# Weights, h and g in SBUF: tiles that begin at one place within 512 bytes, or at several

## The chip, the cores and the metric

The kernel runs on one core of one Trainium2 chip. The metric is the device time of one execution in microseconds, the median of several runs. A profiled execution is one run that the hardware profiler recorded; it has its own time.

## The reference: what is computed

One decoder layer on a sequence of 512 tokens with 1024 channels, in float32:

```
h = modulate(rmsnorm(x, g_ffn1), sh1, sc1)
x = x + 0.5 * gt1 * (silu(h @ w1_gate) * (h @ w1_up)) @ w1_down        # 1024 -> 2816 -> 1024
h = modulate(rmsnorm(x, g_mix), sh2, sc2)
x = x + gt2 * mixer(h)            # one input projection, convolution and sparse attention, one output projection
h = modulate(rmsnorm(x, g_ffn2), sh3, sc3)
x = x + 0.5 * gt3 * (silu(h @ w2_gate) * (h @ w2_up)) @ w2_down
out = rmsnorm(x, g_final)
```

The nine vectors sh, sc and gt come from `silu(c) @ w_ada`, 37.7 MB of weights for one vector c. Almost all the arithmetic is in the two feed-forward parts.

## The kernel before, in words

Activations stand transposed: channels on the 128 partitions, the 512 tokens along the row. Every float32 product is made from float32r parts. A weight block w is split into `whi` (rounded) and `wlo` (the rest), an activation into `hhi` and `hlo`, or `ghi` and `glo` behind the gate. `mm3` (L280) then issues three matmuls for each half of the tokens: hi by hi, low activation by hi weight, hi activation by low weight. Each one has 128 columns of weights to load and 256 columns of activations to stream, and each has its own weight load.

Weights come in units of 1024 columns, 4096 bytes a partition. A unit lands in one of four `raw` tiles, ScalarE rounds it into `whi` (L372), VectorE or GpSimd subtracts to make `wlo` (L361). There are four pairs `whi0..3`, `wlo0..3` (L333), taken in turn. Two further pairs, `whik` and `wlok` (L591), are allocated in the pool of a feed-forward part behind g and hold its last two units. In the mixer the last two units are held in `PT` tiles instead. h is eight pairs of 512 columns, 2048 bytes a partition (L513); g is eleven such pairs (L587).

`project` goes through the eight channels' blocks d of h with one unit of weights: six matmuls for d = 0, six for d = 1, and so on. `part` does the same over the eleven blocks of g, with a unit change every eight. The same weight tile therefore stands against each h tile in turn.

Tiles are laid into a partition's row one after the other in the order in which they are declared. All of these have sizes that are multiples of 512 bytes, so all weights begin at one place within 512 bytes, all h tiles at one place, and all g tiles at one place. Between the weights and h, `cact`, `mod`, `am` and `gb` (L416 to L419) take 112 float32, 448 bytes. Within 512 bytes, h then begins 64 bytes before the place of the weights. As the program is laid out: weights at byte 448, h, g, `whik` and `wlok` at 384, the first four `PT` at 256 and a fifth at 160.

The order of the instructions on each engine is settled when the program is built, by a planner (`Plan`, with costs such as `c_mm3`) that knows nothing of addresses. In the first feed-forward part the 56 tiles of `w_ada` are loaded as well (`araw`), and VectorE adds them up (L871).

Of the kernel before, what the change touches and what calls it, by code (L numbers as in the profile page):

```python
# [10 lines left out]
F32 = mybir.dt.float32  # L11
F32R = mybir.dt.float32r
# [7 lines left out]
P = 128  # L20
T = 512
D = 1024
DK = D // P
F = 2816
FK = F // P
FH = FK // 2
# [7 lines left out]
UNIT = 1024  # L34
# [26 lines left out]
N_RAW, N_W, N_SCR = 4, 4, 6  # L61
# [74 lines left out]
class Plan:  # L136
# [12 lines left out]
    def go(self, rank, task):  # L149
        self.n += 1  # L150
        self.step([rank, self.n, task, [self.at], None], None)
# [8 lines left out]
    def give(self, slots, i, at=None):  # L160
        slots.idle.append((*(at or self.at), i))
        able = [w for w in slots.waiters if w[4] < len(slots.idle)]
        if able:
            w = min(able, key=lambda w: w[:2])
            slots.waiters.remove(w)
            self.step(w, self.take(slots, w))
# [52 lines left out]
def c_act(n):  # L219
    return ACT, 0.1 + 0.84e-3 * n  # L220


def c_tt(n):
    return DVE, 0.07 + 1.04e-3 * n


def c_stt(n):
    return DVE, 0.13 + 1.04e-3 * n
# [14 lines left out]
def c_mm3(n):  # L243
    return PE, 3 * max(n / 2370, 0.105)
# [11 lines left out]
def tile_hymba_layer(ctx: ExitStack, tc: tile.TileContext, xT, pos, cols_d, con_d, wa0, wa1, f1a, f1b, f1d,  # L256
# [3 lines left out]
    const = ctx.enter_context(tc.tile_pool(name="const", bufs=1))  # L260
# [12 lines left out]
    small_of = [const.tile([P, 3, NB, 2], F32, name=f"v{i}") for i in range(8)]  # L273
    small = Slots(range(8))


    def mm(o, lhsT, rhs, start, stop):
        nc.tensor.matmul(o, lhsT, rhs, start=start, stop=stop)  # L278

    def mm3(o, w, x_, start, stop):  # L280

        n = o.shape[-1]
        wide = n == T and x_[0].shape[-1] == T
        halves = HALVES if wide else (slice(0, n),)
        for ts in halves:
            x0, x1 = (x_[0][:, ts], x_[1][:, ts]) if wide else x_
            o_ = o[:, ts] if wide else o
            mm(o_, w[0], x0, start and ts is halves[0], False)
            mm(o_, w[0], x1, False, False)
            mm(o_, w[1], x0, False, stop and ts is halves[-1])  # L290
# [39 lines left out]
    units += ffn_units(f2a, f2b, f2d)  # L330

    raw_of = [const.tile([P, UNIT], F32, name=f"raw{i}") for i in range(N_RAW)]
    whi_of = [const.tile([P, UNIT], F32R, name=f"whi{i}") for i in range(N_W)]  # L333
    wlo_of = [const.tile([P, UNIT], F32R, name=f"wlo{i}") for i in range(N_W)]
    raws, ws = Slots(range(N_RAW)), Slots(range(N_W))
    loaded, made = [Event() for _ in units], [Event() for _ in units]
    raw_at, w_at = {}, {}
# [40 lines left out]
    def take_unit():  # L378
        used[0] += 1
        return used[0] - 1  # L380

    def cols(u, j, n=P):
        i = w_at[u]
        return whi_of[i][:, j * n:(j + 1) * n], wlo_of[i][:, j * n:(j + 1) * n]

    def free_unit(u):
        give(slots_of.get(u, ws), w_at[u])
# [122 lines left out]
            if self.uses[i] == DK and self.copied is None:  # L510
                give(banks, self.bank[i])

    hhi = [const.tile([P, T], F32R, name=f"hhi{d}") for d in range(DK)]  # L513
    hlo = [const.tile([P, T], F32R, name=f"hlo{d}") for d in range(DK)]

    def h_of(d, ts=FULL):
        return hhi[d][:, ts], hlo[d][:, ts]
# [17 lines left out]
    def residual(d, b, gate, ts, norm):  # L535
        n = ts.stop - ts.start
        yield c_stt(n)
        nc.vector.scalar_tensor_tensor(x[d][:, ts], bank_of[b][:, ts], gate, x[d][:, ts], op0=OP.mult, op1=OP.add)  # L538
        give(banks, b)
        yield from norm.add(d, ts)  # L540

    def project(b):

        u = take_unit()
        yield made[u]
        for d in range(DK):
            yield c_mm3(T)
            mm3(bank_of[b], cols(u, d), h_of(d), d == 0, d == DK - 1)
        free_unit(u)
# [34 lines left out]


    def ffn(s, gp, accs, norm, end):
        ghi = [gp.tile([P, T], F32R, name=f"ghi{k}") for k in range(FH)]  # L587
        glo = [gp.tile([P, T], F32R, name=f"glo{k}") for k in range(FH)]
        sg_of = [gp.tile([P, T], F32, name=f"sg{k}") for k in range(2)]
        for k in range(KEEP[s]):  # L590
            whi_of.append(gp.tile([P, UNIT], F32R, name=f"whik{k}"))  # L591
            wlo_of.append(gp.tile([P, UNIT], F32R, name=f"wlok{k}"))
            give(kept[s], len(whi_of) - 1)
        sgs, gs = Slots(range(2)), [Slots([k]) for k in range(FH)]
        g_in = [Event() for _ in range(FK)]
        gate = [mod[:, 3 * s + 2, d:d + 1] for d in range(DK)]
        at = {}

        def glu(f, bg, bu):
            k = yield sgs  # L600
            yield c_act(T)
            nc.scalar.activation(sg_of[k], bank_of[bg], AF.Silu)
            give(banks, bg)
            q = yield scr
            yield c_tt(T)
            nc.vector.tensor_mul(scr_of[q], sg_of[k], bank_of[bu])  # L606
            give(banks, bu)
            give(sgs, k)
            j = yield gs[f % FH]
            yield c_act(T)  # L610
            nc.scalar.activation(ghi[j], scr_of[q], AF.Copy)  # L611
            yield c_tt(T)
            nc.vector.tensor_sub(glo[j], scr_of[q], ghi[j].bitcast(F32))  # L613
            give(scr, q)
            done(g_in[f])

        def part(half, d, b, ts, keep=False):
            for k in range(FH):
                n = d * FH + k
                if (half, n // 8) not in at:  # L620
                    at[half, n // 8] = take_unit()
                u = at[half, n // 8]
                yield made[u]
                yield g_in[half * FH + k]
                yield c_mm3(ts.stop - ts.start)
                mm3(bank_of[b][:, ts], cols(u, n % 8), (ghi[k][:, ts], glo[k][:, ts]), k == 0, k == FH - 1)
                if n % 8 == 7 and not keep:
                    free_unit(u)
                if half == 0 and d == DK - 1:
                    give(gs[k], k)  # L630

        def first_half(d, b):
            yield c_stt(T)
            nc.vector.scalar_tensor_tensor(x[d], bank_of[b], gate[d], x[d], op0=OP.mult, op1=OP.add)
            give(banks, b)

        def main():
            for f in range(GRP):
                go(R_GLU, glu(f, accs[2 * f], accs[2 * f + 1]))
            for f in range(GRP, FK):  # L640
                if f == FH:
                    for d in range(DK):
                        b = yield banks
                        yield from part(0, d, b, FULL)
                        if d == 0:
                            yield mod_in[3 * s + 2]
                        go(R_X, first_half(d, b))
                bg = yield banks
                yield from project(bg)
                bu = yield banks  # L650
                yield from project(bu)
                go(R_GLU, glu(f, bg, bu))
            for d in range(DK - 2):
                b = yield banks
                yield from part(1, d, b, FULL)
                go(R_X, residual(d, b, gate[d], FULL, norm))
            for ts in HALVES:
                for d in (DK - 2, DK - 1):
                    b = yield banks
                    yield from part(1, d, b, ts, True)  # L660
                    go(R_X, residual(d, b, gate[d], ts, norm))
            for n in range(8, FH):
                free_unit(at[1, n])
            done(end)

        go(R_MAIN, main())
# [289 lines left out]
    with tc.tile_pool(name="g0", bufs=1) as gp:  # L956
        go(R_ADA, ada_loads())
        go(R_ADA, ada_sums())
        go(R_TAB, rope_tables())
        parts = start_builds(1, norm)  # L960
        ffn(0, gp, accs, norm, end)
        plan.run(end)
        plan.run(mod_in[8])
        plan.run(tables_in)
# [3 lines left out]
    with ExitStack() as mixer:  # L968
# [634 lines left out]
        n = 0  # L1603
# [105 lines left out]
    with tc.tile_pool(name="g2", bufs=1) as gp:  # L1709
# [54 lines left out]

        squared = norm.squared
        ffn(2, gp, accs, norm, end)
        for d in range(DK):
            go(R_Y, final(d))
# [130 lines left out]
```

## Time and profile before

| | |
|---|---|
| three runs | 1066.27, 1082.69, 1066.21 us (median 1066.27) |
| profiled execution | 1077.18 us, of it 1075.4 us from the first to the last instruction (the span) |
| TensorE busy (PE) | 1054.2 us, 98% of the span, 8753 matmuls |
| weight loads (PEld) | 1009.8 us, 94%, 8753 loads |
| VectorE, ScalarE, GpSimd | 606.0, 408.7 and 51.2 us |
| granted TensorE clock | 0.991 of full speed over the span |

PE rows are matmuls, PEld rows weight loads, which run beside them. A matmul is pipelined: it lasts longer than the distance to the next one's start, so the pace of a dense stretch is read from starts, as time over number, and a busy share of 98% does not say that the array could not go faster.

### The profile page before, as it was taken

What the parts mean: (1) busy time and instruction counts of PE and PEld (TensorE: products, weight loads), DVE (VectorE), ACT (ScalarE), POOL (GpSimd) and SP (SyncE); (2) the same over time, 40 slices, a digit from 0 to 9 for tenths busy, and PEclk for the clock granted to TensorE, in tenths of its full rate; (3) what the DMA queues carried; (4) which work ended last, traced back from release to release, by engine and by line L of the source; (5) the groups of instructions that cost most, each with busy time, mean ns of one, the idle gap of its engine ahead of it and who ended that gap; (6) DMA issues with size and microseconds to landing.
All of it is one profiled execution on the core that took longest, in us unless ns stands there. A gap on an engine that the chain in (4) does not pass through costs nothing.

```text
span 1075.4 us, 20561 instructions
## 1 busy us (share of the span) xinstructions
PE 1054.2 (98%) x8753; PEld 1009.8 (94%) x8753; DVE 606.0 (56%) x1069; ACT 408.7 (38%) x713; POOL 51.2 (5%) x47
## 2 busy tenths in 40 slices
PE   8999999999999999999999999999999999999997
PEld 5899999999999999998887789999999999999997
DVE  4988888833333347699787786744333333233334
ACT  4552222222222224458566775333222122222321
POOL 0310100000000001021001010000000000000000
PEclk8999999999999999999999999999999999999999
DMA  9669999422232231344201014133233322322202
GB/s 336 250 217 324 326 322 323 150 99 99 99 99 99 93 89 48 122 125 160 80 18 37 1 29 130 45 118 118 83 95 99 98 84 94 99 99 85 93 21 79
DMA packets 40732, 134.02 MB, mean 125 GB/s; under 512 B 4704, under 2 KB 8032, under 8 KB 40000
## 3 DMA queue, kind: packets, MB, share of 16 engines
q1 hardware_dynamic: 40640, 132.71, 37.0%
q8 instruction: 68, 1.11, 0.4%
q14 instruction: 24, 0.20, 0.1%
HBM read 130.14 MB, written 2.10 MB: 123 GB/s over the span
## 4 chain that ended last, share of the span: by engine, by line
PE 80%; DVE 10%; DMA 6%; issue 2%; ACT 1%; SPq 0%; DVEq 0%; ACTq 0%
PE b L278 77%; DMA araw<-in_wa_dram 6%; DVE ada L871 3%; PE b L1402 2%; DVE wlo L361 2%; DVE afirst L742 1%; DMA wfirst<-in_wa_dram 1%; DVE glo L613 1%; DVE s L525 1%; ACT whi L372 0%; PE b L1297 0%; DVE s L1045 0%; DVE s L606 0%; DVE swp L1048 0%; DVE afirst L739 0%
## 5 line engine op out<-in xcount | busy, mean ns | idle before, releaser
L278 PE MATMUL b<-hhi,whi 128*128 128x256 f32 x1824 | 515.8, 283 | 0.0
L278 PE MATMUL b<-hlo,whi 128*128 128x256 f32 x1824 | 509.2, 279 | 0.6 <-DVE hlo L531 0.6
L278 PE MATMUL b<-hhi,wlo 128*128 128x256 f32 x1824 | 508.7, 279 | 0.0
L372 ACT ACTIVATE whi<-raw 128x1024 fp32r<-128x1024 f32 (+3 forms) x176 | 178.2, 1013 | 461.4 <-issue 250.3
L278 PEld LDWEIGHTS b<-hhi,whi 128*128 128x128 f32 x1824 | 343.3, 188 | 7.6 <-issue 6.7
L278 PEld LDWEIGHTS b<-hlo,whi 128*128 128x128 f32 x1824 | 346.5, 190 | 1.1 <-DVE hlo L531 1.0
L278 PEld LDWEIGHTS b<-hhi,wlo 128*128 128x128 f32 x1824 | 343.5, 188 | 0.0
L361 DVE TENSOR_TENSOR wlo<-raw,whi 128x1024 fp32r<-128x1024 f32 (+3 forms) x162 | 191.1, 1180 | 223.8 <-ACT whi L372 223.5
L278 PE MATMUL b<-ghi,whi 128*128 128x256 f32 x672 | 188.0, 280 | 0.0
L278 PE MATMUL b<-ghi,wlo 128*128 128x256 f32 x672 | 187.3, 279 | 0.0
L278 PE MATMUL b<-glo,whi 128*128 128x256 f32 x672 | 187.3, 279 | 0.0
L278 PEld LDWEIGHTS b<-glo,whi 128*128 128x128 f32 x672 | 127.6, 190 | 0.0
L278 PEld LDWEIGHTS b<-ghi,whi 128*128 128x128 f32 x672 | 126.2, 188 | 0.8 <-issue 0.8
L278 PEld LDWEIGHTS b<-ghi,wlo 128*128 128x128 f32 x672 | 126.3, 188 | 0.0
L606 DVE TENSOR_TENSOR s<-sg,b 128x512 f32<-128x512 f32 x44 | 30.0, 685 | 102.1 <-PE b L278 101.4
L871 DVE SCALAR_TENSOR_TENSOR ada<-araw,cact,ada 128x1024 f32<-128x1024 f32 x49 | 63.5, 1296 | 16.8 <-DMA araw<-in_wa_dram 16.2
L361 POOL TENSOR_TENSOR wlo<-raw,whi 128x768 fp32r<-128x768 f32 (+2 forms) x14 | 32.2, 2299 | 213.5 <-ACT whi L372 213.5
L538 DVE SCALAR_TENSOR_TENSOR x<-b,mod,x 128x512 f32<-128x512 f32 (+1 forms) x30 | 19.1, 643 | 40.8 <-PE b L278 40.7
L456 ACT ACTIVATE s<-x 128x256 f32<-128x256 f32 (+1 forms) x41 | 19.4, 491 | 54.8 <-DVE x L538 52.8
L611 ACT ACTIVATE ghi<-s 128x512 fp32r<-128x512 f32 x44 | 27.1, 620 | 15.5 <-DVE s L606 15.5
L529 ACT ACTIVATE hhi<-s,mod 128x256 fp32r<-128x256 f32 (+1 forms) x42 | 20.9, 534 | 31.2 <-DVE s L525 25.6
L613 DVE TENSOR_TENSOR glo<-s,ghi 128x512 fp32r<-128x512 f32 x44 | 32.1, 734 | 0.0
(238 smaller groups left out, 963.7 us busy)
## 6 DMA issues: line engine op xcount, KB each, us to landing
araw<-in_wa_dram SPq DMA_DIRECT2D x56, 512.0 KB
raw<-in_f1b_dram SPq DMA_DIRECT2D x38, 512.0 KB
raw<-in_f2b_dram SPq DMA_DIRECT2D x38, 512.0 KB
raw<-in_f1d_dram SPq DMA_DIRECT2D x22, 512.0 KB
raw<-in_f2d_dram SPq DMA_DIRECT2D x22, 512.0 KB
raw<-in_wib_dram SPq DMA_DIRECT2D x14, 512.0 KB
wfirst<-in_wa_dram SPq DMA_DIRECT2D x5, 1024.0 KB
raw<-in_wc_dram SPq DMA_DIRECT2D x8, 512.0 KB
```

Of the source, the lines that this page charges most:

```text
L278: nc.tensor.matmul(o, lhsT, rhs, start=start, stop=stop)
L361: (nc.vector if e == DVE else nc.gpsimd).tensor_sub(wlo_of[j][:, :n], raw_of[i][:, :n], whi_of[j][:, :n].bitcast(F32))
L372: nc.scalar.activation(whi_of[j][:, :n], raw_of[raw_at[u]][:, :n], AF.Copy)
L456: nc.scalar.activation(o[:, ts], x[d][:, ts], AF.Square)
L525: nc.vector.scalar_tensor_tensor(t, x[d][:, ts], am[:, s, d:d + 1], rb(), op0=OP.mult, op1=OP.mult)
L529: nc.scalar.activation(hhi[d][:, ts], t, AF.Identity, bias=sh)
L538: nc.vector.scalar_tensor_tensor(x[d][:, ts], bank_of[b][:, ts], gate, x[d][:, ts], op0=OP.mult, op1=OP.add)
L606: nc.vector.tensor_mul(scr_of[q], sg_of[k], bank_of[bu])
L611: nc.scalar.activation(ghi[j], scr_of[q], AF.Copy)
L613: nc.vector.tensor_sub(glo[j], scr_of[q], ghi[j].bitcast(F32))
L871: nc.vector.scalar_tensor_tensor(a, w, cact[:, k:k + 1], a, op0=OP.mult, op1=OP.add)
L1402: nc.tensor.transpose(pt[:, w:w + P], Pr[t][:, kb * P:(kb + 1) * P], ident)
```

## The change

A function `lag` allocates a tile of n float32 that nothing reads or writes. 16 of them, 64 bytes, are put behind each of the first three pairs of weights, behind each pair of h, and behind every second pair of g. Pairs are now declared together, hi and then low.

```diff
+    def lag(n, pool=const):
+
+        pool.tile([P, n], F32, name=f"lag{next(lags)}")
+
+    lags = iter(range(100))
...
-    whi_of = [const.tile([P, UNIT], F32R, name=f"whi{i}") for i in range(N_W)]
-    wlo_of = [const.tile([P, UNIT], F32R, name=f"wlo{i}") for i in range(N_W)]
+    whi_of, wlo_of = [], []
+    for i in range(N_W):
+        for o, name in ((whi_of, "whi"), (wlo_of, "wlo")):
+            o.append(const.tile([P, UNIT], F32R, name=f"{name}{i}"))
+            if i < N_W - 1 and name == "wlo":
+                lag(16)
...
-    hhi = [const.tile([P, T], F32R, name=f"hhi{d}") for d in range(DK)]
-    hlo = [const.tile([P, T], F32R, name=f"hlo{d}") for d in range(DK)]
+    hhi, hlo = [], []
+    for d in range(DK):
+        hhi.append(const.tile([P, T], F32R, name=f"hhi{d}"))
+        hlo.append(const.tile([P, T], F32R, name=f"hlo{d}"))
+        lag(16)
...
-        ghi = [gp.tile([P, T], F32R, name=f"ghi{k}") for k in range(FH)]
-        glo = [gp.tile([P, T], F32R, name=f"glo{k}") for k in range(FH)]
+        ghi, glo = [], []
+        for k in range(FH):
+            ghi.append(gp.tile([P, T], F32R, name=f"ghi{k}"))
+            glo.append(gp.tile([P, T], F32R, name=f"glo{k}"))
+            if k % 2:
+                lag(16, gp)
```

As the program is laid out, in bytes within 512:

| tiles | before | now |
|---|---|---|
| whi, wlo of slots 0, 1, 2, 3 | 448 for all | 448, 0, 64, 128 |
| hhi, hlo of d = 0 to 7 | 384 for all | 64, 128, 192, 256, 320, 384, 448, 0 |
| ghi, glo of k = 0, 1; 2, 3; ... 10 | 384 for all | 64, 128, 192, 256, 320, 384 |
| whik, wlok | 384 | 384 |
| PT (first four; fifth) | 256; 160 | 448; 352 |

No instruction is added, removed or moved on any engine or queue: every engine's list is the same, row for row, with the same waits; line numbers alone differ (L278 becomes L284).

## Rows read from the trace of the kernel before

**Rows 1.** The page: busy time of each engine, with share and instructions.
```profile
PE 1054.2 (98%) x8753; PEld 1009.8 (94%) x8753; DVE 606.0 (56%) x1069; ACT 408.7 (38%) x713; POOL 51.2 (5%) x47
```

**Rows 2.** Chain of waits, pieces: start us, length us, what, how many instructions.
```profile
198.23 207.10 PE b L278 x1823
...
415.67 46.05 PE b L278 x393
...
656.24 31.61 PE b L278 x275
...
696.36 364.83 PE b L278 x3098
```

**Rows 3.** Stages A:B: PE, PEld, DVE, ACT, POOL busy (instructions), clock, DMA share, GB/s.
```profile
60.00:200.00 140.00, 135.12 (x1194) 130.93 (x1194) 116.84 (x125) 41.08 (x56) 6.17 (x2) 1.00 0.87 306
200.00:380.00 180.00, 180.00 (x1591) 180.00 (x1590) 70.40 (x80) 51.99 (x64) 0.00 (x0) 1.00 0.29 97
...
696.00:1061.00 365.00, 365.00 (x3102) 365.00 (x3101) 128.86 (x157) 101.74 (x132) 0.00 (x0) 1.00 0.28 87
```

**Rows 4.** Groups, PE, 200 to 380 us: out<-in, shapes, count, busy us, mean ns.
```profile
L278 PE MATMUL b<-hhi,whi 128*128 128x256 f32 x352 | 97.2, 276 | 0.0
```

**Rows 5.** The same view, PE, 700 to 1040 us.
```profile
L278 PE MATMUL b<-hhi,whi 128*128 128x256 f32 x679 | 190.8, 281 | 0.0
```

**Rows 6.** Timeline, PE, first feed-forward part: start us, length us, instruction.
```profile
299.75 0.28 PE L278 MATMUL b<-hhi,whi 128*128 128x256 f32 x1
...
302.81 0.28 PE L278 MATMUL b<-hhi,whi 128*128 128x256 f32 x1
```

**Rows 7.** Timeline, PE, the kept units behind g.
```profile
395.93 0.28 PE L278 MATMUL b<-ghi,wlok 128*128 128x256 f32 x1
...
397.49 0.28 PE L278 MATMUL b<-ghi,whik 128*128 128x256 f32 x1
```

**Rows 8.** Timeline, PE, mixer's end: weights in PT tiles.
```profile
677.18 0.28 PE L278 MATMUL b<-hhi,PT 128*128 128x256 f32 x1
...
679.79 0.28 PE L278 MATMUL b<-hlo,PT 128*128 128x256 f32 x1
```

**Rows 9.** Timeline, PE, value products: h is the loaded operand, 280 columns stream.
```profile
443.75 0.29 PE L278 MATMUL b<-whi,hhi 128*128 128x280 f32 x1
...
456.08 0.28 PE L278 MATMUL b<-hhi,whi 128*128 128x256 f32 x1
```

**Rows 10.** Timeline, PE, around a stop at 415 us; in brackets idle time and releaser.
```profile
414.35 0.28 PE L278 MATMUL b<-hhi,wlo 128*128 128x256 f32 x1
...
414.71 0.28 PE L278 MATMUL b<-hhi,wlo 128*128 128x256 f32 x1
415.23 0.43 PE L498 MATMUL b<-con,v 128*128 128x128 f32 x2 [0.24 <-DVE v L411]
...
416.44 0.28 PE L278 MATMUL b<-hhi,wlo 128*128 128x256 f32 x1
...
416.78 0.28 PE L278 MATMUL b<-hhi,wlo 128*128 128x256 f32 x1
```

**Rows 11.** Groups, PE, 480 to 655 us.
```profile
L278 PE MATMUL b<-hhi,wlo 128*128 128x256 f32 x192 | 53.6, 279 | 0.0
```

**Rows 12.** Instructions of tile wlok: durations ns min/median/max, first and last start us.
```profile
L278 PE MATMUL b<-ghi,wlok x32: 279/283/283, 394.9 to 409.2; 128*128 128x256 f32 x32
L361 DVE TENSOR_TENSOR wlok<-raw,whik x2: 1214/1216/1219, 377.3 to 379.1; 128x1024 fp32r<-128x1024 f32 x2
```

**Rows 13.** The page's costliest groups: the subtraction that makes wlo.
```profile
L361 DVE TENSOR_TENSOR wlo<-raw,whi 128x1024 fp32r<-128x1024 f32 (+3 forms) x162 | 191.1, 1180 | 223.8 <-ACT whi L372 223.5
```

**Rows 14.** Chain, 60 to 200 us: one of its longer pieces.
```profile
113.12 6.25 DMA araw<-in_wa_dram
```

**Rows 15.** Timeline, PEld: a weight load beside the matmuls of rows 6.
```profile
299.87 0.19 PEld L278 LDWEIGHTS b<-hhi,wlo 128*128 128x128 f32 x1
```

## The prediction, as put on record before the result

> **What bounds the kernel.** Start with the busy times [rows 1]: PE is busy for 98% of the span, weight loads for 94%, no other engine for more than 56%. A busy share of PE does not say at what pace matmuls go, so the next view is the chain of waits [rows 2]: a piece of 364.83 us with 3098 matmuls, the second feed-forward part, and one of 207.10 us with 1823, most of the first. Both are matmul after matmul with no wait between. Divided out, one matmul takes 117.76 ns in the later piece and 113.60 in the earlier. They are of one shape, 128 loaded and 256 streamed columns, and mostly of the same tiles.
>
> [...] The timelines show the pace itself. In the first part 27 steps take 3.06 us, 113.3 ns each [rows 6]. The mean length of a matmul tells the same without counting: 276 ns there and 281 in the second part [rows 4, 5], so the length grows with the step, by about one ns a ns. And when the first part reaches the kept units, 13 steps take 1.56 us, 120.0 ns each [rows 7], with 283 ns as their median length [rows 12]. Nothing differs there but the tiles in which the weights lie.
>
> So there are three paces, 113.3, about 117.8 and 120.0. A weight load runs beside each matmul: one begins at 299.87 us [rows 15], where the second matmul of rows 6 begins by its step, and lasts 0.19 us. Both read SBUF at once, and the table of places tells what may part the paces. Call distance the place of the loaded weights minus the place of the streamed tile, within 512 bytes. It is 64 in both feed-forward parts with the usual weights, 0 with the kept ones. At 64 there are two paces, and which one holds depends on what went before: around 415 us, three steps take 0.36 us before a stop of PE, 120 by these rounded starts, and after it three take 0.34 us, 113 [rows 10], with the same tiles at the same places.
>
> **What other distances cost, from rows.** With weights in PT tiles the distances are 384 and 288: 22 steps take 2.61 us, 118.6 ns each [rows 8]. In the value products h is loaded and 280 columns stream, at distances 448, 352 and 256 (blocks of 280 columns begin 1120 bytes apart): 96 steps take 12.33 us, 128.4 ns each [rows 9]. At the best pace 280 columns would take 113.3 x 280/256 = 123.9, so these lose 4.5, and I set them at 113.3 + 4.5 = 117.8 for 256 columns. With 120.0 at distance 0, the mean of the three is 118.8. No row at a distance other than 64 holds 113.3 for long.
>
> **What the change does.** No instruction is added or moved; only addresses are. By the table of places now, the distance of slot s against h tile d is 64 x (s - d - 2) within 512. As d goes from 0 to 7 it takes all eight values, each for six matmuls, whatever the slot. Distance 64, where 113.3 is to be had, comes once in eight; for g against the usual slots, 3 times in 44. For the others I take 118.8, which gives 7/8 x 118.8 + 1/8 x 113.3 = 118.1 ns for a dense matmul. This is an estimate, and the number on which all rests. The bounds: 120.0, the worst pace of a row, and 115.7, halfway from 118.1 to 113.3, if the distances that no row shows (128, 192, 320) turn out clean.
>
> The sum, against the profiled execution of 1077.18 us (values at the bounds in brackets):
> - Second feed-forward part: 3098 x (118.1 - 117.76) = +1.1 us [rows 2] (-6.4 to +6.9). It goes at a disturbed pace already.
> - First part from 198 us: 1823 x (118.1 - 113.60) = +8.2 us [rows 2] (+3.8 to +11.7). This is the largest term.
> - Mixer: of the 393 matmuls from 415.67 us, 96 are value products and take 12.33 us; the other 297 take 33.72, 113.5 each, and lose 297 x 4.6 = +1.4. The 275 from 656.24 us take 114.9 each and lose +0.9. In between, 577 matmuls of h have a mean length of 279 ns [rows 11], about 116 by the lengths above: 577 x 2.1 = +1.2. Together +3.5 (0 to +5.6).
> - From 60 to 200 us: 1194 matmuls, at most 1194 x 4.8 = +5.7. But PE is idle for 140.00 - 135.12 = 4.88 us of this stage, DMA is 87% busy [rows 3], and the chain runs through loads of w_ada, such as one of 6.25 us [rows 14]. A slower PE uses up its idle time first. I take +1.0; without this cover it would be +5.7.
> - VectorE's subtraction for wlo also reads two tiles whose distance changes. It takes 1180 ns as a mean over its shapes [rows 13] and 1216 for a kept unit, whose parts lie 64 apart [rows 12]: some 36 ns either way, on an engine that is busy 129 of 365 us in the second part [rows 3]. Nothing, since PE covers it; in the 60 to 200 us stage, with some 25 of them, +-0.9 us.
> - The pads take about 1 KB of a row and no time.
>
> Together +13.8, so **1091 us**. At the bounds the sums are 1075 and 1107.
>
> **Against the median.** The profiled execution lies 10.9 us over the median, and two of the runs lie 16.4 apart. The second part alone, at 113.3 instead of 117.76, would be 3098 x 4.46 = 13.8 us shorter: about what separates them. I read the fast runs as ones that kept the clean pace longer. With distances that change every six matmuls neither pace can hold for long, so fast and profiled executions should meet, and I subtract nothing. If the 10.9 us are the profiler's own instead, the forecast would be 1080.
>
> [...] In the rows the pace follows the tiles' places, 113.3 against 120.0. [...]
>
> **Rivals.**
> - *Places don't matter.* The paces come from something that lasts, as the stop at 415 us suggests (same tiles, new pace), and the kept units are slow by what else is special in them. Then the change does nothing: 1066 to 1077, by the pace that a run falls into. Against it: the pace turns to 120.0 at once with the kept units. Chance 0.09.
> - *Spreading helps: not slower.* Reads that meet at one fixed distance keep meeting, since a late load finds the next matmul in the same way; a new distance every six matmuls breaks this, and each group starts clean. Then 113.3 becomes the rule: -13.8 in the second part, -1.6 in the 577 matmuls of the mixer, about -1 elsewhere: 1061. It decides if five or more of eight distances are clean. For it: the 117.8 pace lasted 365 us without recovering. Against it: distances 0, 256, 288, 352, 384 and 448 all show losses. Chance 0.10, of it 0.03 for a pace clearly under 113.3, for which no row of float32r speaks.
> - *A milder loss, or the profiler's share.* A mean of 115.7, or the 10.9 us: 1075 to 1087. Chance 0.20.
> - *A harsher loss.* Each change of distance adds a transient and the mean is 120 or more: 1100 to 1107. Chance 0.12.
> - *The pads are not there.* A tile that nobody uses might get no room; but the laid-out addresses show them. Under 0.01, within the first rival.
>
> **The numbers.** The forecast, 1088 to 1099, has 0.49. Two per cent of the median, about what a measurement of this kernel can tell from no change, is 1087.6 upward and 1044.9 downward. Slower by more: 0.49 and 0.12, 0.61. Faster by more: 0.03. Within: 0.36. The range from 1071 to 1104 leaves out the helpful case, part of the first rival and the top of the harsh one, just under 0.2.
>
> **What would show it.** In the profile after, the mean length of a matmul on hhi and whi from 200 to 380 us should rise from 276 to about 281, the first part's chain piece from 207 to about 215 us, while the second part stays near 366. Starts should show steps that differ from block to block of d, with the 113s near distance 64. The 60 to 200 us stage should end as before, with less idle PE. I am wrong if both parts come out at 276 ns, or if the second part alone changes. The weakest step is the mean of 118.1, from three mixtures of distances, none of them steady at a single unseen one.

## The result, and the profile after

The changed kernel takes **1090.59 us** (median of four runs, 1089.62 to 1091.92). The kernel before, on the same chip, ran in 1066.27, 1082.69, 1066.21 and 1067.24 us, median 1066.76. The ratio is 1.0226, with a 95% interval of 1.0206 to 1.0246: slower by 2.3%. The forecast was 1091. The ratios here leave out runs of a kernel that lie over 1.5% above its fastest, such as that of 1082.69; the experiments tell what such runs of the kernel before are.

The profiled execution took 1089.62 us, 12.4 more than that of before. The page, busy time of each engine, answers to [rows 1]:

```profile
PE 1069.2 (98%) x8753; PEld 1024.9 (94%) x8753; DVE 606.1 (56%) x1069; ACT 408.9 (38%) x713; POOL 50.8 (5%) x47
```

As many instructions as before, PE busy for 15.0 us longer at the same share, VectorE and ScalarE unchanged. The chain of waits of the changed kernel (start us, length us, what, how many) shows where the time lies:

```profile
201.09 214.00 PE b L284 x1823
...
668.54 32.51 PE b L284 x275
709.60 364.03 PE b L284 x3098
```

The counts are those of [rows 2], so each piece is the same work at another pace. The first part has gone from 113.60 to 117.39 ns a matmul, +6.90 us. The second part goes at 117.50 instead of 117.76, -0.80. The piece of 275 has +0.90. The first part's piece starts 2.86 us later. Between its end and the 275, the stretch has grown from 250.91 to 253.45, +2.54. With these, 12.4 us of span are accounted for.

The stages (from : to, length, then PE, PEld, DVE, ACT and POOL busy with their instructions, clock, DMA share, GB/s) answer to [rows 3]:

```profile
60.00:200.00 140.00, 137.13 (x1176) 132.82 (x1174) 115.25 (x119) 41.02 (x56) 5.82 (x2) 1.00 0.86 305
200.00:380.00 180.00, 180.00 (x1536) 180.00 (x1535) 67.64 (x81) 47.50 (x58) 0.00 (x0) 1.00 0.28 94
696.00:1061.00 365.00, 365.00 (x3107) 364.93 (x3107) 134.60 (x179) 104.16 (x138) 0.00 (x0) 1.00 0.28 87
```

The granted clock is 1.00 of full speed in each of these stages, as in [rows 3], where the two parts go at 113.60 and 117.76 ns [rows 2]: it does not part the paces. From 200 to 380 us PE is busy throughout in both kernels, but gets through 1536 matmuls where it did 1591. The groups of PE in the two parts (200 to 380, then 700 to 1040 us; the last two numbers before the bar's idle time are busy us and mean ns) give the lengths:

```profile
L284 PE MATMUL b<-hhi,whi 128*128 128x256 f32 x352 | 98.7, 280 | 0.0
...
L284 PE MATMUL b<-hhi,whi 128*128 128x256 f32 x704 | 197.8, 281 | 0.0
```

276 has become 280, and 281 has stayed [rows 4, 5]: the two parts now go alike.

### The profile page after: what moved, and what is told of

Same layout as the page of the kernel before. It is cut to its first block, busy times and chain, and to the rows that moved or that the text cites. A ratio compares the mean times of both kernels' runs of the same rounds, so it can differ in the third digit from the quotient of the medians.

```text
span 1087.8 us, 20561 instructions
## 1 busy us (share of the span) xinstructions
PE 1069.2 (98%) x8753; PEld 1024.9 (94%) x8753; DVE 606.1 (56%) x1069; ACT 408.9 (38%) x713; POOL 50.8 (5%) x47
## 4 chain that ended last, share of the span: by engine, by line
PE 83%; DVE 7%; DMA 7%; issue 2%; ACT 0%; SPq 0%; DVEq 0%; ACTq 0%
PE b L284 80%; DMA araw<-in_wa_dram 6%; DVE ada L888 3%; PE b L1419 2%; DVE wlo L371 1%; DVE afirst L759 1%; DMA x<-in_xT_dram 1%; DVE s L538 0%; PE b L1314 0%; DVE glo L630 0%; DVE s L623 0%; DVE afirst L756 0%; DVE v L409 0%; DVE afirst L751 0%; PE b L1264 0%
## 5 line engine op out<-in xcount | busy, mean ns | idle before, releaser
L284 PE MATMUL b<-hhi,whi 128*128 128x256 f32 x1824 | 519.8, 285 | 0.0
L284 PE MATMUL b<-hlo,whi 128*128 128x256 f32 x1824 | 512.1, 281 | 0.5 <-DVE hlo L544 0.5
L284 PE MATMUL b<-hhi,wlo 128*128 128x256 f32 x1824 | 511.3, 280 | 0.0
L284 PEld LDWEIGHTS b<-hhi,whi 128*128 128x128 f32 x1824 | 344.3, 189 | 7.6 <-issue 6.7
L284 PEld LDWEIGHTS b<-hlo,whi 128*128 128x128 f32 x1824 | 344.6, 189 | 1.1 <-DVE hlo L544 0.9
L284 PEld LDWEIGHTS b<-hhi,wlo 128*128 128x128 f32 x1824 | 344.2, 189 | 0.0
L284 PE MATMUL b<-ghi,whi 128*128 128x256 f32 x672 | 189.4, 282 | 0.0
L284 PE MATMUL b<-glo,whi 128*128 128x256 f32 x672 | 188.5, 281 | 0.0
L284 PE MATMUL b<-ghi,wlo 128*128 128x256 f32 x672 | 188.3, 280 | 0.0
L284 PEld LDWEIGHTS b<-ghi,whi 128*128 128x128 f32 x672 | 126.8, 189 | 0.8 <-issue 0.8
L284 PEld LDWEIGHTS b<-glo,whi 128*128 128x128 f32 x672 | 126.7, 188 | 0.0
L284 PEld LDWEIGHTS b<-ghi,wlo 128*128 128x128 f32 x672 | 126.6, 188 | 0.0
```

## The experiments

All are timed on chips beside the kernel before, in three rounds. The runs of the kernel before that the ratios are taken against are a mix of some near 1066 us and some near 1080, so the lengths of the chain's pieces carry the argument, not the ratios. In the quoted expectations, letters name theories: A is the one behind the forecast, that the distance between loaded and streamed tile sets the pace; C, that a change of distance itself costs; A2 is A as mended after the first four runs, with odd multiples of 64 bytes as the distances that can be fast.

**One steady distance at a time.** A single unused tile behind the weights of the kernel before moves h and g away from them, so that one distance holds throughout. Nothing else changes. It has 16 float32 for distance 0, 64 for 320 and 96 for 192.

```diff
     wlo_of = [const.tile([P, UNIT], F32R, name=f"wlo{i}") for i in range(N_W)]
+    const.tile([P, 16], F32, name="lag")
```

Distance 0:

> The kernel before with one pad of 64 bytes between the weights and h, so that the distance (place of the loaded weights minus place of the streamed tile, within 512 bytes) is 0 for every unit instead of 64; nothing else moves against each other. Theory A (the distance sets the pace): the kept units, at distance 0, went at 120.0 ns, so both feed-forward parts go at 120 ns, mean matmul length 283 ns, second part's chain piece 3098 x 120 = 372 us, time about 1061 + 6068 x 6.7 ns = 1102 us (1098 to 1107). Theory B (places don't matter, paces are states that a run falls into): 1066 to 1083 as before. Theory C (the changed kernel lost by changes of distance from block to block, not by the distances): with one fixed distance the pace is 113.3 or 117.8, 1061 to 1088 us.

1104.98 us (1102.40 to 1108.47), ratio 1.0267 [1.0194, 1.0341]. Its chain of waits:

```profile
201.46 218.67 PE b L278 x1823
...
716.43 371.66 PE b L278 x3098
```

119.95 and 119.97 ns a matmul, the 120.0 of the kept units [rows 7], now in all of the kernel. One unused tile of 64 bytes does that. Places decide, and the rival that they don't matter falls; so does C's account of this run, by which a fixed distance goes at 113.3 or 117.8.

Distance 320:

> As the last, with a pad of 256 bytes: distance 320 for every unit, the kept units stay at 0. In the changed kernel's trace single blocks of h at distance 320 went at 113 ns, better than the other distances. Theory A: 113.3 ns in both feed-forward parts, mean length 276 ns, second part 3098 x 113.3 = 351 us, time 1061 to 1066 us, with a smaller spread of runs than before if this distance has only one pace. Theory B: 1066 to 1083. Theory C: 113.3 or 117.8 by the state, 1061 to 1088.

1080.21 us (1068.66 to 1090.01), ratio 1.0021 [0.9962, 1.0079]. Its chain:

```profile
202.15 207.10 PE b L278 x1823
...
700.35 364.83 PE b L278 x3098
```

To the hundredth the lengths of [rows 2]: 113.60 and 117.76. One clean pace throughout, as A expects, was not found; 320 behaves as 64 does.

Distance 192:

> As the last, with a pad of 384 bytes: distance 192 for every unit. In the changed kernel's trace blocks at 192 went at 117 to 119 ns without any at 113. Theory A: 117.8 ns throughout, mean length 281 ns, second part 365 us, time 1061 + 6068 x 4.5 ns = 1088 us (1085 to 1091), although the distance never changes. Theory B: 1066 to 1083. Theory C: 1061 to 1083, the loss of the changed kernel is gone.

1077.61 us (1075.56 to 1080.07), ratio 1.0033 [0.9992, 1.0074]. I had expected 117.8 everywhere, and missed:

```profile
201.54 214.73 PE b L278 x1823
...
710.61 351.31 PE b L278 x3098
```

Now the first part goes at 117.79 and the second at 113.40. Both paces exist at this distance too, the other way round.

The same pad ahead of the weights moves weights, h and g together and leaves the distance at 64:

```diff
+    const.tile([P, 16], F32, name="lag")
     whi_of = [const.tile([P, UNIT], F32R, name=f"whi{i}") for i in range(N_W)]
```

> The kernel before with the 64 byte pad ahead of the weights: weights, h, g and all behind them move on by 64 bytes together, distance 64 as before, every absolute place other than before. Theory A: as before, two paces (113.3 and 117.8), runs between 1062 and 1083, median about 1067. A rival, D (the absolute place of a tile counts, weights at 0 or h at 448 are good or bad by themselves): another pace in both parts, over 1085 if 448 was a good place for weights. Theory B: as before.

1075.34 us (1066.98 to 1087.94), ratio 1.0002 [0.9941, 1.0064]:

```profile
199.95 214.78 PE b L278 x1823
...
705.51 351.33 PE b L278 x3098
```

Moving all places together by 64 bytes leaves the two paces as they were, 117.82 and 113.40 ns here, and D falls; three of the ten runs lie above the 1083 expected. The two paces have changed places once more. Which part gets which pace is not a property of the part, then. The times of the kernel before fit this. Beside these four it ran 25 times: 7 runs took 1065.58 to 1070.30 us, 17 took 1076.67 to 1085.70, one 1150.35 at a granted clock of 0.848; the median was 1080.39. The clock does not part the two clusters: it was 0.987 to 0.993 in the one and 0.987 to 0.994 in the other. The second part alone at the other pace is worth 364.83 - 351.32 = 13.5 us, the first 214.75 - 207.10 = 7.7. The first of these is about the gap between the two clusters, and near the 10.9 us by which the profiled execution lay over the median. That the runs near 1066 us have the fast pace in both parts is not shown: no trace of one was kept.

**Other steady distances**, with pads of 112, 8 and 120 float32 in the same place: 128, 32 and 96.

> The kernel before with a pad of 448 bytes between the weights and h: distance 128 for every unit. Steady distances so far: 0 gave 120.0 ns only; 64, 192 and 320 gave 113.3 or 117.8, by the stage and the run. Theory A2 (only the distance within 128 bytes counts: 0 is bad, 64 has two paces): 128 is as 0, 120 ns throughout, mean length 283 ns, second part 372 us, 1100 to 1108 us. Theory A1 (the place within 512 counts, 0 alone is that bad): 113.3 to 117.8 ns, 1062 to 1088 us.

Distance 128: 1097.51 us (1094.21 to 1099.62), ratio 1.0263 [1.0184, 1.0342].

```profile
204.44 216.33 PE b L278 x1823
...
715.96 367.63 PE b L278 x3098
```

> The kernel before with a pad of 32 bytes between the weights and h: distance 32 for every unit. No run shows a distance between 0 and 64. Theory A2, if the loss shrinks evenly from 0 to 64 within 128: between 113.3 and 120, mean length 277 to 282 ns, 1075 to 1095 us. If only the 64 byte piece counts (A3: 32 shares pieces with 0 and with 64 half the time): about 117 to 119 ns, 1085 to 1097 us. If a part of a piece is enough: one pace of 113.3, 1061 to 1064 us, with little spread, which would be the better version.

Distance 32: 1095.85 us (1094.61 to 1099.41), ratio 1.0256 [1.0178, 1.0333].

```profile
203.56 215.73 PE b L278 x1823
...
716.86 366.53 PE b L278 x3098
```

> The kernel before with a pad of 480 bytes between the weights and h: distance 96 for every unit. Theory A2: the mirror of 32 within 128, so either the same pace as there or, if it matters which operand runs ahead, the other side of 64: one of the two lies under 117 ns and one over. Times 1061 to 1097 us; the two together tell whether the bistable pace at 64 can be made a single one.

Distance 96: 1095.49 us (1090.84 to 1099.22), ratio 1.0245 [1.0163, 1.0326].

```profile
200.61 216.31 PE b L278 x1823
...
712.10 367.52 PE b L278 x3098
```

In all three the pieces go at 118.3 to 118.7 ns, in both parts alike, and the times keep away from 1066. No theory of the three had all of this. At 128, A2 expects 120 ns and 1100 us or more, A1 at most 117.8 ns and 1088 us: both miss. At 32 the pace is where A3 has it, and 96 is alike within 0.4 ns, as the mirror wants. The fast pace was not seen at these distances. Of the seven steady ones tried, 64, 192 and 320 have it at times, and 0, 32, 96 and 128 never did.

**Is it the bad distances or the changing?** The changed kernel with pads of 128 bytes, and behind h only after every second pair, visits 64, 192, 320 and 448 alone:

```diff
-                lag(16)
+                lag(32)
...
-        lag(16)
+        if d in (1, 3, 5):
+            lag(32)
...
-                lag(16, gp)
+                lag(32, gp)
```

> The changed kernel with pads of 128 bytes instead of 64 (behind h d = 1, 3 and 5 alone, for room): the distance still changes from block to block and from unit to unit, over 64, 192, 320 and 448, but is never a multiple of 128, except for some products of kept units. Theory A2: blocks differ only by multiples of 128, so this behaves as the kernel before, with paces of 113.3 and 117.8 by stage and run, 1062 to 1086 us. Theory C (changes of distance cost by themselves): about as the changed kernel, 1088 to 1092 us. Theory A1 with 64 as the one good place of eight: 117 to 118 ns, 1085 to 1090 us.

1088.12 us (1086.99 to 1088.54), ratio 1.0175 [1.0084, 1.0266]:

```profile
203.32 213.44 PE b L284 x1823
...
709.68 362.69 PE b L284 x3098
```

117.08 and 117.07 ns. The distance changes every twelve matmuls of h here, instead of every six. Three of the four distances reached the fast pace when steady (448 was not tried alone), yet nearly the whole loss is there, 2.5 us short of the changed kernel's. Changing among distances that can be fast costs about as much as visiting the others: at a change the matmuls are mostly left at the slow pace. That speaks for C, and against the part of A2 that lets these four do as the kernel before. A1 with 64 as the one good place gives this time too, but the steady runs at 192 and 320 rule it out.

**Half of the pads each.** Without the pads behind h and g, the distance is steady for a unit of h, 48 matmuls, at 384, 448, 0 or 64 by slot:

```diff
-        lag(16)
...
-            if k % 2:
-                lag(16, gp)
```

> The changed kernel with the pads behind the weights alone; all h and g tiles lie at one place. The distance is then steady for a whole unit (48 or more matmuls): 384, 448, 0 and 64 for slots 0 to 3. Theory A2 (the distance within 128 decides: 0 is slow, 64 has two paces, and a slow pace once entered holds): 120 at 384 and 0, 117.8 at 448 and 64, mean 118.9, mean length 282 ns, about 1095 us. Rival F (each new unit at an odd multiple of 64 falls back to 113.3): mean 116.7, mean length 280 ns, 1081 to 1085 us. Theory B: 1066 to 1086.

1093.53 us (1093.16 to 1094.09), ratio 1.0255 [1.0234, 1.0276]:

```profile
200.47 216.00 PE b L284 x1823
...
710.88 366.79 PE b L284 x3098
```

118.49 and 118.40 ns. At the slow pace throughout, the steady runs would give (118.7 + 117.8 + 120.0 + 117.8)/4 = 118.6, an estimate that takes 384 for 128 and 448 for 64. The starts of this trace, put beside the laid-out addresses, bear it out: 119.8 ns at distance 0, 118.6 at 384, 117.4 at 64 and 117.5 at 448 (mean of steps up to 135 ns). So even 48 matmuls at a distance that can be fast did not bring the fast pace back, but for a few. The 1095 that A2 expects is near, and F falls.

Without the pads behind the weights, the distance changes with d alone:

```diff
-            if i < N_W - 1 and name == "wlo":
-                lag(16)
```

> The changed kernel with the pads behind h and g alone; all weights lie at one place, except the kept units. The distance still goes through all eight values as d goes from 0 to 7, as in the changed kernel. Theory A2 and C alike: the loss of the changed kernel in full, 117.5 ns per dense matmul, mean length 280 to 281 ns, 1088 to 1092 us. If the change of place from slot to slot had a part of its own in the loss: clearly under 1086 us.

1088.91 us (1085.60 to 1090.74), ratio 1.0208 [1.0178, 1.0238]:

```profile
202.41 213.28 PE b L284 x1823
...
709.69 362.66 PE b L284 x3098
```

116.99 and 117.06 ns. The pads behind h and g alone give nearly all of the loss, those behind the weights alone a little more than all of it; the halves don't add.

**Half as many loads.** If the loss comes once with each weight load, 512 streamed columns for each load should halve it. In the kernel before, and then in the changed kernel, `mm3` takes all tokens at once:

```diff
-        halves = HALVES if wide else (slice(0, n),)
+        halves = (FULL,) if wide else (slice(0, n),)
```

> The kernel before with matmuls of 512 streamed columns instead of two of 256 where h or g has all 512 tokens, so half as many weight loads; same places, distance 64. In the rows of before 512 column matmuls last 385 to 388 ns where 256 column ones last 276, some 110 ns more. Theory G (the loss is paid once for each weight load that runs beside a stream): 222 to 229 ns per 512 columns, 111 to 114.5 per 256, 1050 to 1068 us with little spread. Rival H (the loss grows with the columns streamed): 226.7 or 235.6 per 512, and 1061 to 1086 us as before.

1082.67 us (1079.36 to 1084.84), ratio 1.0150 [1.0118, 1.0182]. Its chain, then its timeline (start us, length us, instruction):

```profile
201.53 212.81 PE b L278 x965
...
706.14 361.56 PE b L278 x1724
```

```profile
299.84 0.39 PE L278 MATMUL b<-hhi,wlo 128*128 128x512 f32 x1
...
302.64 0.39 PE L278 MATMUL b<-hhi,wlo 128*128 128x512 f32 x1
```

Twelve steps take 2.80 us, 233 ns each, 116.7 for 256 columns: between the two paces. The second 256 columns, which have no load of their own, cost 233.3 - 117.8 = 115.5 ns or more, an estimate that gives the first 256 with theirs no more than the slow pace: about as much as the first, so G falls. (The 385 to 388 ns of the expectation are the shortest nine of 80 such matmuls in the trace of before; the others last up to 502.) The time is in H's range, but H expects two paces and there is one. Both parts lie between their fast and slow lengths (207.10 and 214.75; 351.32 and 364.83), and the runs lie together.

> The changed kernel with matmuls of 512 streamed columns in the same way. Theory G: the loss by distance is paid half as often, so the difference to the last kernel is at most half of the 24 us between the changed kernel and the fast runs of before, 1055 to 1076 us. Rival H: 235 ns per 512 columns and 1086 to 1092 us, as the changed kernel.

1081.22 us (1079.83 to 1082.92), ratio 1.0140 [1.0116, 1.0164]:

```profile
202.44 211.50 PE b L284 x965
...
706.78 360.13 PE b L284 x1724
```

Both expectations miss: the time is above G's 1076 us and below H's 1086. With 512 columns to a load the two kernels take the same, 1081.22 and 1082.67 us, and the pads cost nothing. This is 9.4 us better than the changed kernel, but no version here beats the kernel before where its runs take 1066.

## Why the prediction was right, point by point

- **Places set the pace.** Shown: distance 0 differs from the kernel before in one unused tile and takes 119.95 ns, distance 192 at its best 113.40.
- **First part, +8.2 us.** It was +6.90: the mean came out at 117.39, not 118.1. This is the mis-sized term, and it is well inside its bounds; how its 118.1 was made up is told below.
- **Second part, +1.1.** It was -0.80, by the same mean, 117.50. That it would hardly move, since the profiled execution already had it at the slow pace, held.
- **Mixer, +3.5.** It was 2.54 + 0.90 = 3.4.
- **60 to 200 us, +1.0.** PE's idle time there fell from 4.88 to 2.87 us, as the cover should. The first part's piece begins 2.86 us later, but this start lies anywhere from 199.95 (first part slow) to 204.44 us in the experiments, and at 202.15 where the first part is fast. I don't count the excess to the change.
- **The subtraction, nothing.** Its mean is unchanged against [rows 13]:

```profile
L371 DVE TENSOR_TENSOR wlo<-raw,whi 128x1024 fp32r<-128x1024 f32 (+3 forms) x162 | 191.2, 1181 | 228.3 <-ACT whi L382 228.1
```

- **Fast and profiled executions meet; subtract nothing.** The four runs lie within 2.3 us, and the profiled one is among them. This step was worth more than the largest term: with the 10.9 us taken off, the forecast would have been 1080. The two paces that swap between the parts, in one kernel and under a shift that leaves the distance alone, fit the reason given for it.

**What was wrong is the make-up of the 118.1.** I took 64 as the one good distance of eight, 113.3 there and 118.8 at the seven others. The starts of the changed kernel's trace, put beside the laid-out addresses, give 116.1 ns at 64 and 117.8 as the mean of the seven others. 192 and 320 hold 113.4 and 113.6 as well when steady, and 64 in the changed kernel holds the fast pace only in some of its blocks. Some starts in the timeline of the changed kernel show this:

```profile
300.27 0.28 PE L284 MATMUL b<-hhi,whi 128*128 128x256 f32 x1
...
300.99 0.28 PE L284 MATMUL b<-hhi,whi 128*128 128x256 f32 x1
...
302.63 0.28 PE L284 MATMUL b<-hhi,wlo 128*128 128x256 f32 x1
...
303.09 0.28 PE L284 MATMUL b<-hhi,whi 128*128 128x256 f32 x1
```

The first two bound a block of six at distance 0: 0.72 us, 120 ns a step. The last two bound the last four steps at distance 320: 0.46 us by these rounded starts, 0.454 in the trace, 113.5 ns a step. Blocks do differ, as predicted, but the good one in this stretch is not at 64: the block at 64 that ends at 300.27 goes at 117.3 ns a step. Over the whole kernel 64 is the second best, after 320 with 115.6. Two errors offset each other: more distances can be fast than I thought, and under change they are fast for less of the time. That their mean came within 0.7 ns of the 118.1 is in part luck. With the steady runs' slow paces at all eight distances the mean would be (120.0 + 3 x 118.7 + 4 x 117.8)/8 = 118.4, an estimate that takes 256 and 384 for 128 and 448 for 64; with the fast pace at the four odd multiples, 116.2. The measured 117.4 to 117.5 is between.

So the harsher-loss rival had a point: change does cost, as the run that visits 64, 192, 320 and 448 alone shows with 117.08 and 117.07 ns. It did not come on top of 118.1, but in place of what the other good distances would have given.

How much slower the change is depends on what it is held against. Against runs of the kernel before near 1066 us it is 2.3%. Against the median of its 25 runs beside the first four experiments, 1080.39 us, the 1090.59, measured apart from them, would be 0.9% more. The change takes away the fast pace, and it costs what the fast pace was worth in a run.

**Open.** Why the distance counts is not shown: the traces have starts and lengths alone. What picks the pace at the start of a stretch, and whether a program can hold 113.4 in every run, is not settled: distances 64, 192 and 320 all show both paces, and nothing that I varied fixed the fast one in both parts. The ten runs at 192 all took 1075.56 to 1080.07 us, where those at 64 and 320 spread over some 20, so at 192 each part may have had the same pace in every run; one was traced.

## What to carry to other kernels

Where a stream of matmuls is bound by TensorE, divide each long piece of the chain by its count before pricing a change: 98% busy hid paces from 113 to 120 ns. Where tiles begin relative to each other had a price here, 113.40 to 119.97 ns a matmul over the long pieces at steady distances, and a steady distance at an odd multiple of 64 bytes was the only kind at which a whole stretch reached the best pace; to spread the places gave it up, for 117.39 and 117.50. Where one kernel's runs fall into clusters, look for one stretch with two paces, and say which cluster a ratio is against.

## What the hardware showed that was not expected

- One kernel with fixed addresses runs its long stretches of float32r matmuls (128 loaded, 256 streamed columns) at 113.4 or 117.8 ns, and a stretch keeps its pace for 350 us. The four traces with a steady odd multiple of 64 (64 twice, 192 and 320) can be cut wherever the distance changes or a step takes over 135 ns. Each leaves 17 unbroken stretches of 30 steps and more, the longest of 3040. Taken twelve steps at a time from its seventh on, every one of them goes at 113.3 or at 117.8 ns from start to end; none changes on the way. So in these traces the pace was settled where a stretch started: around the stop of [rows 10] it is 117.8 ns from 409.3 us on, behind the kept units, and 113.3 from 415.62 us on, behind the stop.
- The distance within 128 bytes tells more than that within 512: 64, 192 and 320 have both paces, 32, 96 and 128 have 118.3 to 118.7 alone, and 0 has 120.0.
- Under changing distances the odd multiples are not alike. Grouping the steps of the changed kernel (those up to 135 ns) by distance, 686 to 1178 steps each, the means are 116.1 ns at 64 and 115.6 at 320, but 117.8 at 192 and 118.0 at 448. Distance 64 mostly comes after 128 there and 320 after 384; 192 comes after 256 and 448 after 0. The run that visits four distances alone has other neighbours (64 mostly after 192, 320 after 448, 192 after 320, 448 after 64) and the same split: 116.2 and 116.3, then 117.6 and 117.8. But 64 after 0, for whole units with the pads behind the weights alone, has 117.4. So the distance does not decide by itself; whether what comes before it or the length of the visit does is not shown.
- With 512 streamed columns to a load both kernels went between twice 113.4 and twice 117.8 in both parts: the kernel before at 233.3 ns, the changed kernel at 230.1 to 233.1 by distance, with 256 the quickest and 0 (230.8) quicker than 64 (231.8). The order of the distances at 256 columns is gone.
